# w2 of both FFNs by blocks: where the kept gates' product, silu and second product are called, and the second block unit of FFN 1

## The chip, the cores and the metric

The kernel runs on one core of one Trainium2 chip. Its metric is the device time of one execution in microseconds (us). Engines are named as in the profile: PE (TensorE, matmuls), DVE (VectorE), ACT (ScalarE), POOL (GpSimd) and SP (SyncE, which here only issues DMA transfers). Each engine works through its own instructions in the order in which the program issues them, and waits where an instruction's inputs or its buffer are not ready.

## The reference

One layer of a streaming encoder on 512 tokens of width 1024, all in float32: an FFN, a mixing block (a recurrent branch and windowed attention, gated), and a second FFN, with a norm ahead of and behind each.

```python
def swiglu(x, w1, w3, w2):
    return (jax.nn.silu(x @ w1) * (x @ w3)) @ w2
...
        f = swiglu(rms_norm(h, ffn1_pre_g[l]), ffn1_w1[l], ffn1_w3[l], ffn1_w2[l])
        h = h + 0.5 * rms_norm(f, ffn1_post_g[l])
        u = rms_norm(h, mix_pre_g[l])
        q, k, v, xr, xg = jnp.split(u @ w_in[l], splits, axis=-1)
...
        h = h + rms_norm(merged @ w_o[l], mix_post_g[l])
        f = swiglu(rms_norm(h, ffn2_pre_g[l]), ffn2_w1[l], ffn2_w3[l], ffn2_w2[l])
        h = h + 0.5 * rms_norm(f, ffn2_post_g[l])
```

The hidden width of an FFN is 2816, that is 22 tiles of 128, numbered f = 0 to 21.

## The kernel before

**Numbers in two parts.** Every float32 operand of a matmul is split into a high part (an ACT copy to the matmul's type) and a low part (source minus high part, on DVE). `split2` (L211) does this, and so do L178 and L179 for a weight tile. A product is then three matmuls: high by high, low weight by high, high weight by low. The high parts stand in the trace as `whi` or `[..]h`, the low parts as `wlo` or `[..]l`.

**Buffers.** Almost all tiles lie in one pool of 42 buffers of 4 KB per partition (`NSLOT`, L1673). A tile that is asked for takes a buffer that another tile leaves, and its first writer waits until that tile's last user is done. Banks for PE's results are 8.

**An FFN, first half (w1 and w3).** In FFN 1 the first tiles f = 0 to 3 (`NC1`) are computed one by one (`single`, L1164), in FFN 2 only 0 and 1 (`NC2`). All later tiles go through `Pairs` (L689): one job handles two tiles of one weight with seven half-size products in place of eight, so with sums of the weight's and the input's blocks made beforehand (`prep`, L706). A job of `Pairs.run` (L755) issues, in this order: product a11 and its copy q1 (L771), hook 1, product s1 and its copy q5 (L774), hook 2, then `last` of the job before (its product a22 and what follows it), product s2 and its copy u (L782), hook 3, product s4, product s3 and its copy v (L804), and in the last job of all a12 (`c11`) at this place. The a22 product of a job adds into the same bank that L804 reads. In the last job the silu of the job before (L785) and `tail` (L787) come right behind hook 3, and `tail` once more (L807) ahead of `c11`.

**The factor of FFN 1.** In FFN 1 the input of w1 and w3 is not yet normed: the factor per token (`Rb`, L1012) is computed beside the first matmuls and multiplied in later. So `last` of a w1 job copies the a22 result (L822), multiplies both tiles by the factor (L823, on DVE) and returns the silu of both tiles (L824, on ACT), which the next job calls. FFN 2's input is normed already: there `last` calls three silus on ACT (L826 to L828) and no product with a factor.

**Kept gates.** In FFN 1 the tiles f = 2 and 3 are done before the factor is there. `keep` (L1182) copies their raw results into a tile `kept`, and three steps are left for later: product with the factor (L1190, DVE), silu (L1191, ACT), and the product of silu and the w3 result (L1195, DVE).

**An FFN, second half (w2).** The hidden tiles 4 to 19 go through `Halves` (L518): w2 is multiplied by blocks, again seven products in place of eight, in 28 units of 12 matmuls (`unit`, L605), four for each of the products m1, m5, m2, m6, m7, m3, m4. `prep` (L573) makes one unit's operands: weights' high part (L591 or L587, ACT) and low part (L596 on DVE, or L593/L587 on ACT with an adding DMA from POOL), the hidden tile's split (L213 on ACT, L214 on DVE), and the sums that later units need (L548 and L551, DVE). The first units are made ready in the last pair job: hooks 1 and 2 and the two calls of `tail` make units 0 to 3. `run` (L636) then does, for each unit u: `prep` up to unit u + 4, the hooks of u, the matmuls of u, and after units 3, 7, 15 and 19 the copy or sum of the banks (`out`, L619; L629 is the ACT copy, L627 the DVE sum). The products m1, m6, m7 and m4 add into the same two banks (`BANK`, L524), so unit 16 waits for the copy after unit 15.

The hidden tiles that are left over, 0 to 3, 20 and 21, are the tail (`TAIL`, L1684): `RAW_TAIL` and `SPLIT_TAIL` (L1692) say at which units their weights are loaded and they and their weights are split, in the order that `TAIL` gives; `H_BACK` brings back the residual tiles h. `tok_gemm` (L366) then adds the tail's products token tile by token tile, in the same order, and norms each token tile (`norms`, L314), whose result is transposed on PE (L343). Ahead of that it asks for the next weights, `raw_xr` in FFN 1 (L413). In FFN 1 the softplus of a small vector (L1121) is hooked to unit 25.

Where the kept steps are called is set by these lines: each entry of `KEPT_AT` (L1685) is a unit, and the step goes ahead of the unit's other hooks.

```python
    for u, fn in zip(KEPT_AT, (gate_kept, swiglu_kept) * (NC1 - NG)):
        half.hooks[u].insert(0, lambda f=NG + KEPT_AT.index(u) // 2, fn=fn: fn(f))
```

Of the kernel before, what the change touches and what calls it, by code (L numbers as in the profile page):

```python
# [12 lines left out]
AF = mybir.ActivationFunctionType  # L13
ALU = mybir.AluOpType
# [37 lines left out]
def hybrid_layer(ctx: ExitStack, tc: tile.TileContext, a: dict, out: bass.AP):  # L52
    nc = tc.nc
    act, dve, pool, pe, sp = nc.scalar, nc.vector, nc.gpsimd, nc.tensor, nc.sync
# [8 lines left out]
    def slot(shape, dt=F32, name="s"):  # L63
        uid[0] += 1
        return sb.tile(shape, dt, tag="slot", name=f"{name}_{uid[0]}")
# [38 lines left out]
    def want(name, tiles):  # L104
        order.extend((name, i) for i in tiles)
# [3 lines left out]
    def want_ffn(na, nb, n):  # L109

        for i in range(n):
            order.extend([(na, i), (nb, i)])
        for i in range(n, FT, 2):
            paired.update(range(len(order), len(order) + 4))
            order.extend([(na, i), (na, i + 1), (nb, i), (nb, i + 1)])

    want_ffn("w1a", "w3a", NC1)
    want("w2a", TAIL)
    order += [("xr", i) for i in range(8)]
# [14 lines left out]
    want_ffn("w1b", "w3b", NC2)  # L134
    want("w2b", TAIL)

    st = {"dma": 0, "split": 0, "get": 0}
    raws, pairs = {}, {}
# [10 lines left out]
    def dma_to(n):  # L149
        while st["dma"] < min(n, len(order)):  # L150
            dma_one(st["dma"])
            st["dma"] += 1
# [11 lines left out]
    def split_to(n):  # L164
        while st["split"] < min(n, len(order)) and st["split"] not in paired:
            k = st["split"]
            dma_to(k + 1)
            r = raws.pop(k)
            if order[k] in BY_DMA:
                nm, i = order[k]  # L170
                pairs[k] = split_dma(r, a[nm][i * P : (i + 1) * P, :])
            else:
                hi = slot([P, D], F32R, name="whi")
                lo = slot([P, D], F32R, name="wlo")
                if order[k] in BY_POOL:
                    pool.tensor_copy(hi, r)
                else:
                    act.activation(hi, r, AF.Copy)  # L178
                dve.tensor_tensor(out=lo, in0=r, in1=f32(hi), op=ALU.subtract)  # L179
                pairs[k] = (hi, lo)  # L180
            st["split"] += 1
# [469 lines left out]
    def blocks(nm, hid, pairs, late, h_src):  # L651

        hooks = {u: [] for u in range(28)}

        def tail_tile(n):
            hid.to(n + 1)
            split_to(st["get"] + n + 1)

        def h_back(t):
            h[t] = slot([P, D], name="h")  # L660
            sp.dma_start(out=h[t], in_=h_src(t))

        for at_, fn in ((RAW_TAIL, lambda n: dma_to(st["get"] + n + 1)), (SPLIT_TAIL, tail_tile), (H_BACK, h_back)):
            for n, u in enumerate(at_):
                hooks[u].append(lambda n=n, fn=fn: fn(n))
        half = Halves(nm, hid, hooks)
        pairs.more = lambda n: half.load(LOAD_PAIRS[n])
        ahead = lambda: half.prep(half.ready + 1)
        end = len(pairs.jobs) - 1
        late[end, 1], late[end, 2] = [ahead], [ahead]  # L670
        pairs.run(ahead, late)
        return half

# [336 lines left out]

    hid, X1 = Hidden(TAIL), {}
    Rb = slot([P, 2, SEQ], name="Rb")  # L1012
# [134 lines left out]
    def uview(hh, th):  # L1147

        return lambda e, k: uT[:, e, 4 * hh + k, th * 256 : th * 256 + 256]
# [9 lines left out]
    def to_uT(src, hh, th):  # L1159
        v = [uT[:, e, 4 * hh : 4 * hh + 4, th * 256 : th * 256 + 256] for e in range(2)]  # L1160
        split2(v[0], v[1], src)
        return uview(hh, th)
# [17 lines left out]
    kept = {}  # L1180

    def keep(u):  # L1182
        f, i = u // 2, u % 2
        if f not in kept:
            kept[f] = slot([P, 2, SEQ], name="kept")
        act.activation(kept[f][:, i, :], ps[u], AF.Copy)

    def gate_kept(f):
        t = kept[f]
        dve.tensor_tensor(out=t[:, 0, :], in0=t[:, 0, :], in1=Rb[:, 0, :], op=ALU.mult)  # L1190
        act.activation(t[:, 0, :], t[:, 0, :], AF.Silu)  # L1191

    def swiglu_kept(f):
        t = kept.pop(f)
# [25 lines left out]
    late = {(0, 1): [lambda: keep(2 * NC1 - 1)], (1, 1): [bias_in], (2, 3): [bias_parts], (3, 1): [bias_rows]}  # L1220
    for i in range(P // 16):
        late[4 + i, 1] = [lambda i=i: bias_spread(i)]

    h.clear()
    half = blocks("w2a", hid, pairs_a, late, lambda t: a["x"][t * P : (t + 1) * P, :])
    X1 = pairs_a = late = None
    for u, fn in zip(KEPT_AT, (gate_kept, swiglu_kept) * (NC1 - NG)):
        half.hooks[u].insert(0, lambda f=NG + KEPT_AT.index(u) // 2, fn=fn: fn(f))
    half.hooks[SOFTPLUS_AT].append(softplus)
    xf = {(hh, th): slot([P, 4, 256], name="xf") for hh in range(2) for th in range(2)}  # L1230
    bs = tok_gemm(
        "w2a", hid, FT, len(TAIL), "ffn1_post_g", 0.5, "mix_pre_g", [("xr", i) for i in range(4)], xf=xf, spill=True, eps=veps, pre=half)
    half = None
# [376 lines left out]

    hid, tn = Hidden(TAIL), []
    X2 = {"b11": uview(0, 0), "b21": uview(1, 0), "b22": uview(1, 1)}
# [38 lines left out]
    late = {(0, 1): [lambda: X2.update(t4=to_uT(tn[3], 0, 1)), tn.clear]}  # L1651
    pairs_b.prep(1, 1)

    half = blocks("w2b", hid, pairs_b, late, lambda t: h_scr[t])
    X2 = pairs_b = None
    tok_gemm("w2b", hid, FT, len(TAIL), "ffn2_post_g", 0.5, None, [], pre=half)

# [23 lines left out]

BY_POOL = {("wg", i) for i in range(2, 8)} | {("wk", 0), ("wk", 1)}

TAIL = (0, 1, 2, 3, 20, 21)  # L1684
KEPT_AT = (15, 17, 18, 19)  # L1685
SOFTPLUS_AT = 25
LEAD = 5
U_SLOTS = 4
# [14 lines left out]
NC1 = 4  # L1703

NG = 2
# [55 lines left out]
```

## Time and profile before

| | before |
|---|---|
| median of 3 runs | 1123.17 us (1122.95 to 1123.32) |
| profiled execution | 1123.3 us |
| its span | 1121.5 us |
| granted clock of PE, mean | 0.990 |
| PE busy | 1101.1 us, 98% |
| DVE busy | 914.2 us, 82% |
| ACT busy | 669.2 us, 60% |
| POOL busy | 390.0 us, 35% |

The span runs from the first to the last instruction; the execution's time has 1.8 us more around it. Busy times are of the whole span: an engine with 82% can still be the one that is late in one stage, so the stage is what has to be read. A view of waits lists who waited for whom; a timeline lists the instructions of a stretch with the idle time before each; a view of windows gives busy time and granted clock of each engine in stretches that one chooses. FFN 1's w2 blocks lie between 237 and 324 us of the span, FFN 2's between 1004 and 1081 us.

### The profile page before, as it was taken

The page shows a single profiled execution, that of the slowest core. Times are in us where ns is not written, and L with a number is a line of the kernel's source. Part 1 is how long each engine was busy: PE and PEld are TensorE (multiplying, and loading weights), DVE is VectorE, ACT ScalarE, POOL GpSimd, SP SyncE. Part 2 cuts the span into 40 slices and gives each one's busy share as a digit, 9 for nine tenths or more (in the row PEclk, how much of TensorE's full clock was granted, in tenths as well). Part 3 has the DMA queues.
Part 4 walks back from the last instruction along what each step waited for, and adds up shares of the span by engine and source line. Part 5 has one row for each costly group of instructions (what it writes and reads, how often), then busy time and mean ns, then how long its engine had stood idle before and what let it go on. Part 6 is the DMA issues. An engine that isn't in the chain of part 4 may idle for free.

```text
span 1121.5 us, 17990 instructions
## 1 busy us (share of the span) xinstructions
PE 1101.1 (98%) x6850; PEld 993.1 (89%) x6850; DVE 914.2 (82%) x1337; ACT 669.2 (60%) x1175; POOL 390.0 (35%) x308
## 2 busy tenths in 40 slices
PE   9999999989799999999999999999999999999997
PEld 7899999978688877899888888888999999998885
DVE  5878999899778978888677866767889989589954
ACT  7755555557646677856556564356555555567821
POOL 0242532202111523033565664010877655602100
PEclk9999999989899999999999999999999999999999
DMA  9235653547762562136222245352323323376731
GB/s 351 101 97 132 149 117 112 177 162 161 176 226 86 177 170 94 57 120 236 99 93 76 94 169 207 105 197 85 141 76 113 113 76 114 111 241 147 190 120 75
DMA packets 52662, 155.41 MB, mean 139 GB/s; under 512 B 5456, under 2 KB 7376, under 8 KB 52576
## 3 DMA queue, kind: packets, MB, share of 16 engines
q1 hardware_dynamic: 42256, 129.57, 32.8%
q0 software_dynamic: 10032, 24.16, 10.7%
q8 instruction: 54, 0.88, 0.3%
q10 hardware_dynamic: 288, 0.52, 0.1%
q14 instruction: 32, 0.26, 0.1%
HBM read 138.52 MB, written 13.62 MB: 136 GB/s over the span
## 4 chain that ended last, share of the span: by engine, by line
PE 93%; DVE 5%; ACT 1%; issue 1%; DMA 0%; DVEq 0%; SPq 0%; ACTq 0%
PE c L683 13%; PE c L684 13%; PE c L685 13%; PE f L224 9%; PE f L225 9%; PE f L226 9%; PE hw L615 4%; PE hw L617 4%; PE hw L616 4%; PE acc L244 2%; PE acc L242 2%; PE acc L243 2%; PE hw L243 1%; PE hw L244 1%; PE hw L242 1%; DVE wlo L596 1%
## 5 line engine op out<-in xcount | busy, mean ns | idle before, releaser
L684 PE MATMUL c<-uT,wlo 128*128 128x256 f32 x516 | 146.0, 283 | 0.0
L685 PE MATMUL c<-uT,whi 128*128 128x256 f32 x516 | 146.0, 283 | 0.0
L683 PE MATMUL c<-uT,whi 128*128 128x256 f32 x516 | 146.0, 283 | 0.0
L683 PE MATMUL c<-Xh,whi 128*128 128x256 f32 x504 | 142.7, 283 | 0.0
L684 PE MATMUL c<-Xh,wlo 128*128 128x256 f32 x504 | 142.6, 283 | 0.0
L224 PE MATMUL f<-uT,whi 128*128 128x512 f32 (+1 forms) x368 | 136.4, 371 | 0.2 <-DVE o L1550 0.2
L225 PE MATMUL f<-uT,wlo 128*128 128x512 f32 (+1 forms) x368 | 134.8, 366 | 0.0
L226 PE MATMUL f<-uT,whi 128*128 128x512 f32 (+1 forms) x368 | 134.8, 366 | 0.0
L685 PE MATMUL c<-Xl,whi 128*128 128x256 f32 x456 | 129.1, 283 | 0.0
L214 DVE TENSOR_TENSOR wlo<-S,whi 128x1024 fp32r<-128x1024 f32 x86 | 118.8, 1381 | 6.8 <-ACT whi L213 3.3
L213 ACT ACTIVATE whi<-S 128x1024 fp32r<-128x1024 f32 x86 | 88.5, 1055 | 30.8 <-DVE S L732 29.7
L684 PEld LDWEIGHTS c<-uT,wlo 128*128 128x128 f32 x516 | 99.0, 192 | 0.2
L683 PEld LDWEIGHTS c<-uT,whi 128*128 128x128 f32 x516 | 99.0, 192 | 0.2
L685 PEld LDWEIGHTS c<-uT,whi 128*128 128x128 f32 x516 | 99.0, 192 | 0.0
L683 PEld LDWEIGHTS c<-Xh,whi 128*128 128x128 f32 x504 | 96.8, 192 | 0.3 <-issue 0.3
L684 PEld LDWEIGHTS c<-Xh,wlo 128*128 128x128 f32 x504 | 96.8, 192 | 0.0
L685 PEld LDWEIGHTS c<-Xl,whi 128*128 128x128 f32 x456 | 87.5, 192 | 0.0
L615 PE MATMUL hw<-whi,uT 128*128 128x512 f32 x192 | 76.0, 396 | 7.0 <-ACT hc L629 7.0
L224 PEld LDWEIGHTS f<-uT,whi 128*128 128x128 f32 x368 | 69.4, 189 | 12.7 <-issue 1.4
L226 PEld LDWEIGHTS f<-uT,whi 128*128 128x128 f32 x368 | 69.4, 188 | 11.5
L225 PEld LDWEIGHTS f<-uT,wlo 128*128 128x128 f32 x368 | 69.4, 189 | 10.8
L1503 POOL TENSOR_SCALAR P<-P,d 128x256 f32<-128x256 f32 (+1 forms) x64 | 62.0, 984 | 45.7 <-DVE d L1501 33.3
(434 smaller groups left out, 3199.3 us busy)
## 6 DMA issues: line engine op xcount, KB each, us to landing
raw_w2a<-in_w2a_dram SPq DMA_DIRECT2D x22, 512.0 KB, 4.1
raw_w1b<-in_w1b_dram SPq DMA_DIRECT2D x22, 512.0 KB, 4.1
raw_w3b<-in_w3b_dram SPq DMA_DIRECT2D x22, 512.0 KB, 4.3
raw_w2b<-in_w2b_dram SPq DMA_DIRECT2D x22, 512.0 KB, 4.5
raw_w3a<-in_w3a_dram SPq DMA_DIRECT2D x21, 512.0 KB, 4.3
raw_w1a<-in_w1a_dram SPq DMA_DIRECT2D x20, 512.0 KB, 4.2
raw_wg<-in_wg_dram SPq DMA_DIRECT2D x16, 512.0 KB, 3.8
h<-in_x_dram SPq DMA_DIRECT2D x8, 512.0 KB, 6.5
```

The costliest lines, as they stand in the source:

```text
L213: act.activation(hi, src, AF.Copy)
L214: dve.tensor_tensor(out=lo, in0=src, in1=f32(hi), op=ALU.subtract)
L224: pe.matmul(ps[:, c0:c1], wh[:, s], h_, start=k == 0 and c0 == 0, stop=False, skip_group_check=True)
L225: pe.matmul(ps[:, c0:c1], wl[:, s], h_, start=False, stop=False, skip_group_check=True)
L226: pe.matmul(ps[:, c0:c1], wh[:, s], l_, start=False, stop=k == KT - 1, skip_group_check=True)
L615: pe.matmul(ps, xs[:, 0, j, c], hi[:, j, :], start=start and j == 0, stop=False, skip_group_check=True)
L616: pe.matmul(ps, xs[:, 0, j, c], lo[:, j, :], start=False, stop=False, skip_group_check=True)
L617: pe.matmul(ps, xs[:, 1, j, c], hi[:, j, :], start=False, stop=u % 4 == 3, skip_group_check=True)
L683: pe.matmul(ps, wh[:, s], xh, start=first, stop=False, skip_group_check=True)
L684: pe.matmul(ps, wl[:, s], xh, start=False, stop=False, skip_group_check=True)
L685: pe.matmul(ps, wh[:, s], xl, start=False, stop=k == 3, skip_group_check=True)
L1503: pool.tensor_scalar(out=pt[:, x, b0:256], in0=pt[:, x, b0:256], scalar1=d[:, x : x + 1], scalar2=None, op0=ALU.mult)
```

## The change

Three edits. The second block unit that FFN 1 prepares inside the last pair job moves from hook 2 to hook 3, that is behind the product with the factor; FFN 2 keeps hook 2. The first product and the silu of a kept gate become two functions, and the six steps of the two kept gates, which were called at units 15, 17, 18 and 19, are called at units 18 and 19 (products with the factor), 21 and 22 (silus), 22 and 23 (second products). The order of the tail, for both FFNs, becomes 0, 1, 20, 21, 2, 3.

```diff
-        late[end, 1], late[end, 2] = [ahead], [ahead]
+        late[end, 1], late[end, 2 if pairs.R is None else 3] = [ahead], [ahead]
...
     def gate_kept(f):
-        t = kept[f]
-        dve.tensor_tensor(out=t[:, 0, :], in0=t[:, 0, :], in1=Rb[:, 0, :], op=ALU.mult)
-        act.activation(t[:, 0, :], t[:, 0, :], AF.Silu)
+        dve.tensor_tensor(out=kept[f][:, 0, :], in0=kept[f][:, 0, :], in1=Rb[:, 0, :], op=ALU.mult)
+
+    def silu_kept(f):
+        act.activation(kept[f][:, 0, :], kept[f][:, 0, :], AF.Silu)
...
-    for u, fn in zip(KEPT_AT, (gate_kept, swiglu_kept) * (NC1 - NG)):
-        half.hooks[u].insert(0, lambda f=NG + KEPT_AT.index(u) // 2, fn=fn: fn(f))
+    for fn, at_ in zip((gate_kept, silu_kept, swiglu_kept), KEPT_AT):
+        for f, u in zip(range(NG, NC1), at_):
+            half.hooks[u].insert(0, lambda f=f, fn=fn: fn(f))
...
-TAIL = (0, 1, 2, 3, 20, 21)
-KEPT_AT = (15, 17, 18, 19)
+TAIL = (0, 1, 20, 21, 2, 3)
+KEPT_AT = (18, 19), (21, 22), (22, 23)
```

## The prediction

> **What bounds the kernel now.** The page's first part puts TensorE (PE) at 1101.1 of the 1121.5 us span; nothing but PE's gaps, and stretches in which PE is slow, can be won. So I read the waits of PE first (who waited <- for whom: total us, times, longest).
>
> ```profile
> PE hw L615 <- ACT hc L629: 7.0, 1, 7.0
> PE c L683 <- ACT ct L804: 3.8, 1, 3.8
> ```
>
> Both lie in FFN 1, where the change acts; FFN 2, with the same code for pairs and blocks, has no such row. I then read the timeline around each. A row is start, duration, engine, line, operation, tiles; the bracket is the idle time before and what ended it. The 7.0 us first:
>
> ```profile
> 287.08 0.69 DVE L1190 TENSOR_TENSOR kept<-kept,Rb 128x512 f32<-128x512 f32 x1
> ...
> 287.81 0.63 ACT L1191 ACTIVATE kept<-kept 128x512 f32<-128x512 f32 x1 [8.78 <-DVE kept L1190]
> 288.34 1.07 ACT L629 ACTIVATE hc<-hw 128x512 f32<-128x512 f32 x2
> ...
> 288.97 0.80 PE L615 MATMUL hw<-whi,uT 128*128 128x512 f32 x1 [6.96 <-ACT hc L629]
> ```
>
> Block unit 16 adds into the banks that L629 copies out after unit 15, so PE must wait for the copy. The copy stands on ACT behind the silu of kept gate 2 (L1191), and this behind its product (L1190), which DVE reaches only after all the work queued before it: ACT idled 8.78 us for it. Unit 15 itself was done at 282.0 (288.97 - 6.96). Now the 3.8 us:
>
> ```profile
> 226.76 0.37 ACT L822 ACTIVATE cc<-c 128x256 f32<-128x256 f32 x1
> 231.59 1.06 ACT L824 ACTIVATE cc<-cc 128x1024 f32<-128x1024 f32 x1 [4.19 <-DVE cc L823]
> ...
> 233.50 0.61 ACT L213 ACTIVATE hx<-hEO 128x512 fp32r<-128x512 f32 x1
> 234.02 0.36 ACT L804 ACTIVATE ct<-c 128x256 f32<-128x256 f32 x1
> ...
> 226.86 1.22 DVE L596 TENSOR_TENSOR wlo<-raw_w2a,whi 128x1024 fp32r<-128x1024 f32 x1
> ...
> 229.74 0.69 DVE L551 TENSOR_TENSOR hEO<-hEO,hEO 128x512 f32<-128x512 f32 x1
> 230.34 1.22 DVE L823 TENSOR_TENSOR cc<-cc,Rb 128x1024 f32<-128x1024 f32 x1
> ...
> 234.43 0.58 PE L683 MATMUL c<-Xh,w 128*128 128x256 f32 x1 [3.82 <-ACT ct L804]
> ```
>
> The last a22 product needs the bank that L804 reads. L804 stands behind the silu L824, this waits for the factor product L823, and L823 stands on DVE behind the four operations of the second block unit (L596 to L551, 226.86 to 230.34), though its last input (L822) was there at 227.1.
>
> An idle PE also loses its clock. The windows give the granted clock as the column before the last two.
>
> ```profile
> 232.60:233.60 1.00, 0.00 (x0) 0.00 (x0) 0.00 (x0) 1.00 (x3) 0.00 (x0) 0.60 0.02 6
> 234.40:239.80 5.40, 5.37 (x19) 4.82 (x20) 5.40 (x9) 3.02 (x4) 0.00 (x0) 0.52 0.19 55
> ...
> 288.90:294.20 5.30, 5.23 (x12) 4.13 (x13) 2.89 (x4) 5.30 (x9) 1.85 (x2) 0.50 0.33 50
> ```
>
> The clock fell 2.2 us into the idle time (0.60 is 0.2 us at 1 and 0.8 at half, from 232.6; idle since 230.6) and stayed at half for some 5.3 us of work after either wait. That is 2.6 us each, beside the waits: 7.0 + 3.8 + 5.2 = 16.0 us is all that lies here.
>
> **The change, part by part.** *Second block unit behind the factor product.* No instruction is added; L591, L213 on ACT and L596, L214, L548, L551 on DVE go from hook 2 to hook 3 of the last pair job, past the a22 product of the job before, its copy L822 and the copy L782; the one load that they bring to SP's queue, the tenth of w2a, feeds unit 8 at the earliest. L823 then starts at about 226.9, when the first unit's DVE work ends, and ends at 228.0. ACT does L782, the moved L591 and L213, L824, the third unit's L591 and L213, L804, back to back from 226.4 (starts lie some 0.1 closer than the durations, so 1.5 for an L591 with its L213 and 1.0 for L824): L804 at 230.7 in place of 234.02, PE's a22 at 231.2. That leaves a wait of 0.5, too short for the clock. Its 12 matmuls took 2.73 at clock 0.52, so 1.4 at 1, and block unit 0 starts at 232.6.
>
> What is late next is DVE. FFN 2 shows it, because there nothing multiplies by the factor and PE does not stop:
>
> ```profile
> 222.02 0.38 ACT L771 ACTIVATE ct<-c 128x256 f32<-128x256 f32 x1 [0.54 <-PE c L685]
> ...
> 993.97 0.38 ACT L771 ACTIVATE ct<-c 128x256 f32<-128x256 f32 x1 [0.54 <-PE c L685]
> ...
> 1022.94 0.39 PE L615 MATMUL hw<-whi,uT 128*128 128x512 f32 x1
> 1023.94 0.50 PE L617 MATMUL hw<-whi,uT 128*128 128x512 f32 x1
> ...
> 1023.20 0.68 DVE L214 TENSOR_TENSOR uT<-hEO,uT 128x512 fp32r<-128x512 f32 x1
> ...
> 1048.31 0.50 PE L615 MATMUL hw<-whi,uT 128*128 128x512 f32 x1
> ...
> 1075.60 1.22 DVE L179 TENSOR_TENSOR wlo<-raw_w2b,whi 128x1024 fp32r<-128x1024 f32 x1
> ```
>
> The last pair jobs start 771.95 us apart (L771). DVE's order from there is FFN 2's, plus one L823 (1.13 from start to start of neighbours). FFN 2's unit 7 got its low part when L214 ended at 1023.88, and its third matmul went at 1023.94; here that is 253.1. PE alone would bring unit 7's third matmul at 232.6 + 7 x 2.72 + 0.45 = 252.1 (2.72 a unit: (321.48 - 294.26)/10, rows below). So DVE takes back 1.0 us over units 5 to 7, in pieces under 1 us. This makes the sum insensitive to the 0.5 above: up to 1 us more there costs nothing.
>
> ```profile
> 260.09 0.39 PE L615 MATMUL hw<-whi,uT 128*128 128x512 f32 x1
> ...
> 294.26 0.40 PE L615 MATMUL hw<-whi,uT 128*128 128x512 f32 x1
> ...
> 321.48 0.39 PE L615 MATMUL hw<-whi,uT 128*128 128x512 f32 x1
> ```
>
> Unit 8 starts at 253.1 + 2.27 = 255.4 where it was 260.09: 4.7 us. *The kept product leaves unit 15.* ACT is then free when unit 15 ends; the copy fits as in FFN 2, where unit 16 (1048.31) began 0.2 after its turn. So unit 16 at 255.4 + 8 x 2.72 + 0.2 = 277.4, unit 17 at 280.1 against 294.26: **14.2 us** up to here. The four kept instructions on DVE (0.6 from start to start) and two on ACT are the same; what hides them is DVE's lead. In FFN 2 unit 27's operands were ready long before its turn:
>
> ```profile
> 1072.65 0.69 DVE L214 TENSOR_TENSOR uT<-hEO,uT 128x512 fp32r<-128x512 f32 x1
> ...
> 1078.39 0.39 PE L615 MATMUL hw<-whi,uT 128*128 128x512 f32 x1
> ```
>
> Moved by 771.95, with 1.13 and three of the kept operations (1.8), L214 ends at 304.3, PE comes at 307.3: 3.0 us of lead, so PE pays nothing in these units; without the lead each kept operation would cost its 0.6. The new waits are harmless: behind a silu on ACT stand a unit's or a tail tile's conversions, but its product was issued three units earlier, and by DVE's order above the two are done near 289 and 292, while ACT comes to the silus at 291 and 293.
>
> *End of the stage.* DVE ends FFN 2's tail at 1076.8; minus 771.95, plus 1.13, plus four kept operations (2.4), plus softplus:
>
> ```profile
> 315.41 0.16 DVE L1126 TENSOR_SCALAR z<-z 128x8 f32<-128x8 f32 x1
> ...
> 320.04 0.70 DVE L1143 TENSOR_SCALAR bxh<-vec 64x8 f32<-64x8 f32 x4
> 320.77 0.69 DVE L214 TENSOR_TENSOR hT<-cc,hT 128x512 fp32r<-128x512 f32 x1
> ...
> 321.49 3.00 SPq L146 DMA_DIRECT2D raw_xr<-in_xr_dram  x3
> ...
> 318.84 1.06 ACT L178 ACTIVATE whi<-raw_xr 128x1024 fp32r<-128x1024 f32 x1 [5.27 <-DMA raw_xr<-in_xr_dram]
> ...
> 326.28 1.07 ACT L178 ACTIVATE whi<-raw_xr 128x1024 fp32r<-128x1024 f32 x1 [0.94 <-DMA raw_xr<-in_xr_dram]
> ...
> 332.56 0.69 DVE L294 TENSOR_TENSOR hc<-hw,hc 128x512 f32<-128x512 f32 x1 [3.35 <-PE hw L244]
> ...
> 339.34 0.75 DVE L333 SCALAR_TENSOR_TENSOR hg<-h,r,bc_mix_pre_g 128x512 f32<-128x512 f32 x1
> ...
> 340.52 1.03 PE L343 MATMUL tr<-ident,hg 128*128 128x128 f32 x8
> ```
>
> Softplus takes 5.3, so DVE ends at 313.7. PE ends unit 27 at 310.0 and wants the last tail tile, now kept gate 3, at 313.4: 0.3 late. DVE thus gains only 8.9 us where PE gains 14.2. The fourth raw_xr load was issued (321.49) when the last tail tile's split freed its buffer (L214, to 321.46); now that is 312.6. From 321.46 it took 7.1 us until DVE had that weight split and was at the first L294 (328.5); so 319.7, and the second L294 at 320.3 against 332.56 - 14.2 = 318.4. The chain to L333 had 0.4 to spare before the transposes (340.09 against 340.52). Loss: 1.5, the 0.3 included.
>
> *The tail's order, in both FFNs.* No instruction more or less; pair 20, 21 is split two places earlier, 2, 3 later, and a buffer comes free at other units. FFN 2 has no PE wait and I take 0. What a changed buffer can do is seen in the block loop's copies (idle before them, and who ended it):
>
> ```profile
> L591 ACT ACTIVATE whi<-raw_w2a 128x1024 fp32r<-128x1024 f32 x24 | 25.2, 1051 | 9.7 <-PE hw L616 3.7 <-PE hw L617 3.4 <-DVE uT L214 1.9
> ```
>
> They wait for buffers, up to 1.9 us at once, so each of these edits may cost or gain about 2 us; I keep both ends.
>
> *A rule beside it.* The Trainium skill (TensorE: Matmul & The Clock Gate, "What's actually happening") says that the clock is halved after an idle window of about 3.4 us and returns after about 3.4 us of work. The rows differ: 2.2 and 5.3. By its 3.4 us of half clock the two recoveries would give 3.4 us and not 5.2, and the forecast would be 1.8 us higher.
>
> **The sum.** 14.2 - 1.5 = 12.7 us. The profiled execution took 1123.3 us (span 1121.5 and 1.8 around it), the median is 1123.17, so the two scales agree to 0.1: **1110.6 us**. All later stages run on PE without a wait worth a row, and move as a whole.
>
> **The rivals.** *The next load is not late* (the fourth raw_xr gets a buffer earlier): nothing of the 1.5 is lost, perhaps also the 1.0 of units 5 to 7 not: 1107.5 to 1109. *The copy stays behind something else.* L629 still stands behind L591 and L213 of unit 19, and L591 there waited for a DVE L214. If its new buffer comes with unit 17's or 18's L214 (278 to 282 in the new times), the copy is 2 to 5 us late, and over 2.2 us the clock's 2.6 comes on top: 1113 to 1118. For it: the 1.9 in the row above; against it: FFN 2, where the same copy waits for PE alone. *The change doesn't do what it says* (the copy or L804 was held by buffers and the named waits only ended last): 1121 to 1125. Against it: the 8.78 and 4.19 name the products. *Slower: loads behind the kept tile.* SP issues in order. If one of the four h loads, and not the fourth raw_xr, gets kept gate 3's buffer, free at 312.6, then eight loads follow from there, one every 2.5 us ((326.28 - 318.84)/3), after 4.8 for the first: 334.8, then 2.9 for both splits and L294: 337.7, 5.1 later than before; less 0.4 spare, plus 2.6 of clock: 7 us slower, 1130. It decides against the change once more than five loads stand behind that buffer. Against it, the h loads were issued 13 us before the last tail tile was split:
>
> ```profile
> 308.07 3.52 SPq L661 DMA_DIRECT2D h<-in_x_dram  x4
> ```
>
> **How the numbers follow.** Forecast (1109 to 1113) 0.62; next load in time 0.12; copy still held 0.15; no effect 0.05; slower 0.06. The range 1107.5 to 1117.5 takes in the first three and their buffer terms, and leaves out about 0.14. A measurement of this kernel tells 0.2%, 2.2 us, from no change. Faster 0.89, within 0.05, slower 0.06.
>
> **What would show it.** Right: neither row of the first fence over 1 us; no window at half clock between 225 and 315; unit 17 at 280; DVE without a gap from 226 to 313; a wait of PE on L343's hg of 1 to 2 us. Wrong: L629 with a long bracket naming DVE; L615 waiting for whi or uT by more than 1 us; raw_xr issued after 315; any new PE wait in FFN 2.

## The result, and the profile after

| | before | after |
|---|---|---|
| median of 4 runs each | 1123.06 us (1122.88 to 1123.32) | 1110.70 us (1110.65 to 1110.95) |
| profiled execution, span | 1123.3, 1121.5 us | 1110.68, 1108.9 us |
| granted clock of PE, mean | 0.990 | 0.998 |
| DVE busy | 914.2 us | 912.5 us |

After takes 0.989 of the time of before (95% interval 0.9873 to 0.9907). Where did 12.6 us of span go? First all the waits of PE in the kernel after (who waited <- for whom: total us, times, longest):

```profile
PE w L990 <- POOL warm L987: 1.1, 1, 1.1
PE hw L243 <- DVE wlo L179: 0.7, 1, 0.7
PE c L683 <- ACT ct L804: 0.3, 1, 0.3
PE hw L616 <- DMA wlo<-in_w2b_dram: 0.3, 1, 0.3
```

The 7.0 us wait is gone and the 3.8 us one is 0.3. The first row lies at the start of the kernel. The second and the last are new: the last tail tile of FFN 1 (a product with kept gate 3), and block unit 23 of FFN 2. Now the timeline of after around both places (start, duration, engine, line, operation, tiles; bracket: idle time before, and who ended it):

```profile
226.91 1.22 DVE L823 TENSOR_TENSOR cc<-cc,Rb 128x1024 f32<-128x1024 f32 x1
228.16 1.06 ACT L824 ACTIVATE cc<-cc 128x1024 f32<-128x1024 f32 x1
230.59 0.36 ACT L804 ACTIVATE ct<-c 128x256 f32<-128x256 f32 x1
231.01 0.39 PE L683 MATMUL c<-Xh,w 128*128 128x256 f32 x1 [0.34 <-ACT ct L804]
232.54 0.40 PE L615 MATMUL hw<-whi,hx 128*128 128x512 f32 x1
...
253.16 0.51 PE L617 MATMUL hw<-whi,uT 128*128 128x512 f32 x1
255.56 0.39 PE L615 MATMUL hw<-whi,uT 128*128 128x512 f32 x1
...
275.33 1.06 ACT L591 ACTIVATE whi<-raw_w2a 128x1024 fp32r<-128x1024 f32 x1 [3.44 <-DVE uT L214]
276.30 0.61 ACT L213 ACTIVATE uT<-hEO 128x512 fp32r<-128x512 f32 x1
276.84 1.28 ACT L629 ACTIVATE hc<-hw 128x512 f32<-128x512 f32 x2
277.49 0.50 PE L615 MATMUL hw<-whi,uT 128*128 128x512 f32 x1
280.35 0.39 PE L615 MATMUL hw<-whi,uT 128*128 128x512 f32 x1
```

The factor product L823 comes right behind the first unit's work, ACT meets no wait before L804, unit 0 starts at 232.54. Unit 7's third matmul goes at 253.16, held back by DVE as in FFN 2, and unit 8 at 255.56. The copy L629 follows L213 with no bracket, and unit 17 is at 280.35: 13.9 us ahead of before. The chain that the prediction feared, a copy behind an L591 that waits for a buffer, is there all the same: L591 waited 3.44 us for DVE's L214, and ACT came to the copy only at 276.84. Unit 16 starts 0.39 us after the matmul before it, where matmuls in a row start 0.23 apart, so 0.16 us was lost. It was near.

The windows of after (stretch, then PE, PEld, DVE, ACT and POOL busy; granted clock; DMA's mean busy share; GB/s):

```profile
225.00:315.00 90.00, 88.70 (x413) 72.87 (x412) 89.18 (x134) 64.99 (x89) 16.49 (x15) 1.00 0.78 212
```

The clock is 1.00 throughout: the half-clock stretches are gone. And DVE is busy for 89.18 of 90 us: it now works nearly without a gap, as the prediction had it.

The end of the stage in after:

```profile
303.08 4.76 SPq L146 DMA_DIRECT2D raw_xr<-in_xr_dram  x3
307.55 0.39 PE L615 MATMUL hw<-whi,uT 128*128 128x512 f32 x1
...
311.24 1.58 DVE L1143 TENSOR_SCALAR bxh<-vec 64x8 f32<-64x8 f32 x4
311.38 2.79 POOL L410 TENSOR_SCALAR bc_mix_pre_g<-bc_mix_pre_g 128x1024 f32<-128x1024 f32 x1 [6.77 <-DMA bc_mix_pre_g<-in_mix_pre_g_dram]
...
313.45 1.22 DVE L179 TENSOR_TENSOR wlo<-raw_w2a,whi 128x1024 fp32r<-128x1024 f32 x1
314.59 4.62 DVE L179 TENSOR_TENSOR wlo<-raw_xr,whi 128x1024 fp32r<-128x1024 f32 x4
314.73 0.50 PE L243 MATMUL hw<-wlo,hT 128*128 128x512 f32 x1 [0.67 <-DVE wlo L179]
319.13 1.28 DVE L294 TENSOR_TENSOR hc<-hw,hc 128x512 f32<-128x512 f32 x2
327.60 1.03 PE L343 MATMUL tr<-ident,hg 128*128 128x128 f32 x8
```

DVE's row is unbroken: softplus, the last tail split, then four splits of the next weights in a row (4.62 us), then the first L294. PE waits 0.67 us at the last tail tile. The transposes start at 327.60 against 340.52: 12.9 us are gained at the end of FFN 1.

One thing in these rows can't be read from the order of the instructions. The four instructions of L1143, the end of softplus, took 0.70 us in before and 1.58 here: one of them, at 311.40, took 1.04 and the others 0.15 to 0.17. It started as POOL began L410 (311.38). Without this 0.88 us the last tail split would end at 313.79, ahead of PE, which comes to it at 313.90 (0.23 after the matmul at 313.67). In three other profiles, too, a DVE instruction beside L410's start is the long one: L1137 with 0.96 us in the whole with less lateness, L214 with 1.47 for 0.69 under the extra DVE operation, L1143 with 1.05 under the fourth low part (these experiments are below). That POOL holds DVE up there is argued from these rows; no run moves L410.

FFN 2 (units 0 and 27) takes 1065.79 - 990.67 = 75.12 us where it took 1078.39 - 1003.85 = 74.54:

```profile
990.67 0.40 PE L615 MATMUL hw<-whi,hx 128*128 128x512 f32 x1
...
1065.79 0.39 PE L615 MATMUL hw<-whi,uT 128*128 128x512 f32 x1
```

```profile
1003.85 0.40 PE L615 MATMUL hw<-whi,hx 128*128 128x512 f32 x1
```

(The second fence is before.) So 12.9 us at the end of FFN 1, less 0.6 in FFN 2, plus 0.3 gained between the two, make 12.6 us, the difference of the spans.

### The profile page after: what moved, and what is told of

It reads as the page before. It is cut to its first block, busy times and chain, and to the rows that moved or that the text cites. A ratio compares the mean times of both kernels' runs of the same rounds, so it can differ in the third digit from the quotient of the medians.

```text
span 1108.9 us, 17987 instructions
## 1 busy us (share of the span) xinstructions
PE 1098.4 (99%) x6850; PEld 989.6 (89%) x6850; DVE 912.5 (82%) x1337; ACT 668.9 (60%) x1175; POOL 389.9 (35%) x308
## 4 chain that ended last, share of the span: by engine, by line
PE 86%; DVE 10%; DMA 2%; issue 1%; ACT 0%; POOL 0%; DVEq 0%; SPq 0%; POOLq 0%; ACTq 0%
PE c L683 12%; PE c L684 12%; PE c L685 12%; PE f L224 9%; PE f L225 9%; PE f L226 9%; DVE wlo L596 2%; PE acc L243 2%; PE acc L244 2%; PE acc L242 2%; DVE uT L214 1%; DVE raw_w2a L548 1%; PE hw L243 1%; PE hw L244 1%; PE hw L242 1%
## 5 line engine op out<-in xcount | busy, mean ns | idle before, releaser
L683 PE MATMUL c<-uT,whi 128*128 128x256 f32 x516 | 146.1, 283 | 0.0
L683 PE MATMUL c<-Xh,whi 128*128 128x256 f32 x504 | 142.8, 283 | 0.0
L214 DVE TENSOR_TENSOR wlo<-S,whi 128x1024 fp32r<-128x1024 f32 x86 | 118.7, 1380 | 8.1 <-POOL OL L1557 4.5
L213 ACT ACTIVATE whi<-S 128x1024 fp32r<-128x1024 f32 x86 | 88.5, 1054 | 31.4 <-DVE S L732 29.7
L683 PEld LDWEIGHTS c<-uT,whi 128*128 128x128 f32 x516 | 99.1, 192 | 0.2
L683 PEld LDWEIGHTS c<-Xh,whi 128*128 128x128 f32 x504 | 96.8, 192 | 0.3 <-issue 0.3
L224 PEld LDWEIGHTS f<-uT,whi 128*128 128x128 f32 x368 | 69.4, 189 | 12.5 <-issue 1.7
L616 PE MATMUL hw<-wlo,uT 128*128 128x512 f32 x192 | 75.2, 392 | 0.4 <-DMA wlo<-in_w2b_dram 0.3
```

What stands on the lines that cost most here:

```text
L213: act.activation(hi, src, AF.Copy)
L214: dve.tensor_tensor(out=lo, in0=src, in1=f32(hi), op=ALU.subtract)
L224: pe.matmul(ps[:, c0:c1], wh[:, s], h_, start=k == 0 and c0 == 0, stop=False, skip_group_check=True)
L616: pe.matmul(ps, xs[:, 0, j, c], lo[:, j, :], start=False, stop=False, skip_group_check=True)
L683: pe.matmul(ps, wh[:, s], xh, start=first, stop=False, skip_group_check=True)
```

## The experiments

The theory: PE is the bound; the two waits and the clock lost in them are all that can be won; once they are gone, DVE sets the pace of units 0 to 7 and of the end of the stage. The rivals: the gains of the edits simply add; the tail's order or the exact units matter; another engine or the transfers, not DVE, are late next. Medians of before in these runs are 1123.42 to 1123.49 (1123.06 in the result), so times can be set beside each other.

**One edit at a time: the hook.** Before, with the second block unit behind the factor product, nothing else:

```diff
-        late[end, 1], late[end, 2] = [ahead], [ahead]
+        late[end, 1], late[end, 2 if pairs.R is None else 3] = [ahead], [ahead]
```

> The kernel before with the hook edit alone (second block unit at hook 3). Theory, DVE sets the pace from the pair jobs' end to the kept product: the 3.8 us wait falls to 0.3 to 0.5 and its half clock goes, but DVE comes to the kept product only 2.1 us earlier (L596 of unit 4 at 240.9 in place of 243.0), so the wait of unit 16 for the copy grows from 7.0 to about 10 and the time is 1121.0. Rival, the waits of PE add: 3.8 + 2.6 of clock are won, 1116.7, and the second wait stays at 7.0.

Measured: 1121.36 us, ratio 0.9983 (0.9973 to 0.9992). Waits of PE and timeline in this kernel:

```profile
PE hw L615 <- ACT hc L629: 9.4, 1, 9.4
```

```profile
285.24 0.67 DVE L1190 TENSOR_TENSOR kept<-kept,Rb 128x512 f32<-128x512 f32 x1
285.95 0.63 ACT L1191 ACTIVATE kept<-kept 128x512 f32<-128x512 f32 x1 [8.77 <-DVE kept L1190]
```

The first wait went to 0.4 us, as forecast, and the second grew from 7.0 to 9.4. PE came earlier to unit 16, but the product L1190 ends a chain on DVE, which came only 1.84 us earlier (287.08 to 285.24). A wait removed upstream is handed to the next one, if that is set by another engine.

**One edit at a time: the kept steps and the tail.** After, with the hook at 2 for both FFNs.

```diff
-        late[end, 1], late[end, 2 if pairs.R is None else 3] = [ahead], [ahead]
+        late[end, 1], late[end, 2] = [ahead], [ahead]
```

> The changed kernel with the hook edit undone (kept steps at separate units and the new tail order alone). Theory: the 7.0 us wait and its 2.6 us of half clock go, the 3.8 us wait stays; DVE's end of the stage comes 2.1 us later than with both edits and costs little, since PE is later too: 1113.7. Rival, the edits add: 12.4 less the first wait's 6.4, so 6.0 us, 1117.1.

Measured: 1118.3 us, ratio 0.9941 (0.992 to 0.9961), but the runs fall into two groups, 1113.7 and 1114.1, and 1118.3 to 1119.5. The profile is of the second:

```profile
PE c L683 <- ACT ct L804: 3.8, 1, 3.8
PE hw L616 <- DMA wlo<-in_w2a_dram: 2.0, 1, 2.0
```

```profile
301.30:303.70 2.40, 0.37 (x2) 0.00 (x0) 2.40 (x5) 0.65 (x2) 0.00 (x0) 1.00 1.03 392
303.70:307.90 4.20, 4.18 (x11) 3.31 (x12) 4.20 (x6) 3.35 (x6) 0.00 (x0) 0.59 1.02 414
```

The 7.0 us wait is gone and the 3.8 us one stands, as it should. A new wait is there: unit 23 needs its low part, which an adding transfer brings, and the DMA engines are full (share 1.03). The wait of 2.0 us costs the clock as well (0.59 in the 4.2 us behind it): units 22 and 23 together take 307.93 - 298.56 = 9.4 us (their first start to unit 24's) and not 2 x 2.72, 3.9 more. Without them the profiled run's 1118.4 would be 1114.5, near the first group; since that group has no profile, that it lacks the wait is argued, not shown.

**One edit at a time: the tail's order.**

```diff
-TAIL = (0, 1, 2, 3, 20, 21)
+TAIL = (0, 1, 20, 21, 2, 3)
```

> The kernel before with the tail's order alone (0, 1, 20, 21, 2, 3 in both FFNs; kept steps and hook as before). Theory: nothing in FFN 1, where the copy's wait is the same, and 0.6 us lost in FFN 2, where the changed kernel's unit 23 waits for its low part's transfer: 1123.7. Rival, the order itself is what relieves the tail: 1 to 2 us won, 1121.5.

Measured: 1122.9 us, ratio 0.9998 (0.9989 to 1.0008). Both old waits stand (7.8 and 3.8 us). FFN 2 takes 1077.72 - 1003.14 = 74.58 us between units 0 and 27, so the 0.6 us that after loses in FFN 2 does not come from the order alone, and my expectation of a loss there failed. The order is worth nothing by itself.

**Is it the product's place or the silu's?** Before, with product and silu parted into two functions, as the change does, and the first product still at unit 15; hook and tail are those of before. Gate 3's product moves from unit 18 to 17, the second products from 17 and 19 to 18 and 20. Of the edit the list of units is shown:

```diff
-KEPT_AT = (15, 17, 18, 19)
+KEPT_AT = (15, 17), (17, 19), (18, 20)
```

> The kernel before with the kept silu alone moved off unit 15: products stay at 15 and 17, silus go to 17 and 19, second products to 18 and 20; old tail order, old hook. Theory, the copy waits because ACT works in order and the silu stands ahead of it: the 7.0 us wait goes although the product stays where it was: 1113.7, as with the kept steps moved late. Rival, DVE's place for the product matters (it now stands before unit 20's work, not behind it): a wait of over 1 us for the copy or for a unit's operands stays, 1116 or more.

Measured: 1115.23 us, ratio 0.9926 (0.9911 to 0.994). The copy in the timeline:

```profile
281.61 1.28 ACT L629 ACTIVATE hc<-hw 128x512 f32<-128x512 f32 x2 [2.56 <-PE hw L617]
287.10 0.68 DVE L1189 TENSOR_TENSOR kept<-kept,Rb 128x512 f32<-128x512 f32 x1
```

The product comes as late as ever (287.10; 287.08 in before), but the copy no longer stands behind its silu and waits for PE alone. So it was ACT's order that cost the 7.0 us: not the product, but what was queued behind the instruction that waited for it. A new wait of 1.4 us, for the low part of unit 23, takes part of it back, and the time is 1.5 us above the forecast of 1113.7.

**The whole with less lateness.** After, with the steps of the previous experiment and the old tail:

```diff
-TAIL = (0, 1, 20, 21, 2, 3)
-KEPT_AT = (18, 19), (21, 22), (22, 23)
+TAIL = (0, 1, 2, 3, 20, 21)
+KEPT_AT = (15, 17), (17, 19), (18, 20)
```

> Hook edit and separate silu together, but the kept steps early (products at units 15 and 17, silus at 17 and 19, second products at 18 and 20) and the tail's old order: the change without its lateness. Theory, what counts is that the silu no longer stands ahead of the copy on ACT; where the product stands among DVE's work is worth nothing to PE: 1110.7, as the whole change, give or take 0.7. Rival, the late kept steps and the new order carry part of the 12.4 us: 1113 or more.

Measured: 1111.09 us, ratio 0.9895 (0.988 to 0.991), the same as after within the intervals. Two things make the result: the hook, and a silu that is not in the copy's way.

**Is DVE the bound?** After, with one more 128x1024 operation on DVE (the maximum of the factor tile with itself, which changes no value) in the last pair job:

```diff
+                    if self.R is not None:
+                        dve.tensor_tensor(out=self.R, in0=self.R, in1=self.R, op=ALU.max)
```

> The changed kernel with one more DVE instruction of 128x1024 (1.13 us from start to start; a maximum of the factor tile with itself, which changes no value) behind the fourth block unit's work. Theory, DVE is what PE now waits for, first in units 5 to 7 and again at the end of the stage: 1.1 us slower, 1111.8, with unit 7 some 1.1 us later. Rival, DVE's work is covered: 1110.7.

Measured: 1112.03 us, ratio 0.9902 (0.9887 to 0.9917); span 1110.1 against 1108.9. In its timeline unit 7's third matmul is at

```profile
254.23 0.50 PE L617 MATMUL hw<-whi,uT 128*128 128x512 f32 x1
```

1.07 us later than in after. A DVE operation there costs its whole length (1.13 us from start to start): DVE sets the pace of units 0 to 7.

**Is the clock's term real?** Before, with 52 idle matmuls of 128x240 on a zero tile between units 15 and 16, in the gap in which PE waits for the copy (the lines that make the tile are not shown):

```diff
+                if u == 15 and self.nm == "w2a":
+                    ps = bank("w")
+                    for _ in range(52):
+                        pe.matmul(ps[:, :240], keep_warm[:, :P], keep_warm, start=True, stop=True)
```

> The kernel before with 52 matmuls of 128x240 on a zero tile into a spare bank between units 15 and 16, some 5.8 us that lie in the 7.0 us wait; they compute nothing that is used. Theory, half of what the wait costs beyond itself is the clock: with PE kept at work unit 16 runs at full clock, 2.6 us faster than before, 1120.6, though PE does more. Rival, unit 16 is slow for another reason (its operands or banks): 1123.2 or more, with starts 0.43 us apart as before.

Measured: 1122.87 us, ratio 0.9994 (0.9985 to 1.0004): the expected gain did not come. The trace says why:

```profile
282.12 5.97 PE L645 MATMUL w<-gap 128*128 128x240 f32 x52
...
289.00 0.53 PE L615 MATMUL hw<-whi,uT 128*128 128x512 f32 x1 [0.91 <-ACT hc L629]
291.92 0.39 PE L615 MATMUL hw<-whi,uT 128*128 128x512 f32 x1
...
310.76 0.50 PE L616 MATMUL hw<-wlo,uT 128*128 128x512 f32 x1 [1.87 <-DMA wlo<-in_w2a_dram]
```

Unit 16 starts where it did (289.00; 288.97) and runs at full clock: unit 17 is at 291.92 and not at 294.26, so the clock's term, 2.3 us, is shown. Unit 23 then waits 1.87 us for its low part, and the clock falls again (0.76 from 310.7 to 317.7). In this execution, at 1124.74 us the slowest of the ten, the clock was won and more than given back 20 us later; that a shorter wait at unit 23 eats the gain in the others is likely, but they have no profile.

**Softplus away from DVE, to POOL.** After, with softplus's small instructions on POOL but for three on DVE:

```diff
-        dve.tensor_tensor(out=z[1], in0=z[1], in1=z[2], op=ALU.mult)
+        pool.tensor_tensor(out=z[1], in0=z[1], in1=z[2], op=ALU.mult)
...
```

> The changed kernel with most of the softplus (all but three of its small instructions, 5 us of DVE) on POOL, which is idle then. Theory, the transposes are late because DVE has the tail's splits, softplus and four weight splits in a row and only then the first norm: the 0.7 us wait of the last tail tile and about 0.4 us before the transposes go: 1109.5. Rival, the load of the next weights is what is late (as I had put it in the prediction): 1110.7.

Measured: 1115.82 us, ratio 0.9934 (0.9919 to 0.9949), 5 us slower than after. It does not answer the question, whether DVE's list is what makes the end late, since it added two waits on DVE and one of PE (3.1 us for hg at the transposes):

```profile
312.85 0.17 DVE L1136 SCALAR_TENSOR_TENSOR z<-z,z 128x8 f32<-128x8 f32 x1 [5.75 <-POOL z L1135]
...
323.94 0.69 DVE L299 SCALAR_TENSOR_TENSOR fg<-hc,bc_ffn_post_g 128x512 f32<-128x512 f32 x1 [3.34 <-DMA bc_ffn_post_g<-in_ffn_post_g_dram]
```

The one step left on DVE waited 5.75 us for POOL, and the transfer L281, which after issues at 299.85, came behind softplus on POOL's queue at 319.84. A step moved to another engine brings that engine's queue with it.

**Softplus earlier on DVE.** After, with Abs and Exp ahead of the Silu table and the 29 DVE instructions in six parts behind pair jobs 4 to 14:

```diff
+    for i in range(6):
+        late[4 + 2 * i, 3] = [lambda i=i: soft_part(5 * i)]
...
-    half.hooks[SOFTPLUS_AT].append(softplus)
```

> The changed kernel with the gate's softplus moved: its Abs and Exp run ahead of the Silu table's load, and its 29 small VectorE instructions go in six parts behind pair jobs 4 to 14 of the third part of FFN 1, so that none of them is left in unit 25 of FFN 1. Theory (VectorE is what the end of FFN 1 waits for): the 0.7 us that the last tail tile waited for VectorE goes, and the tail splits and the work on the residual start earlier; of the 6.0 us of softplus only what reached PE is won, 0.7 + 0.4 us: about 1109.5 us. Rival (VectorE has no room behind the pair jobs, or the loads of the residual end the stage): 1110.7 us or more.

Measured: 1111.79 us (1110.72 to 1112.34), ratio 0.9892 (0.9878 to 0.9907); the total missed, while the tail did what the theory says: no wait there, and the transposes come 329.14 - 310.10 = 19.04 us behind unit 27's start, as in before (340.52 - 321.48); in after it is 20.05. So what made DVE late at the end, the lengthened instruction of L1143 included, is worth 1.0 us. It was lost again at a place that I had not thought of, and in part at units 21 and 23 (0.56 and 0.36 us for low parts):

```profile
34.84 1.28 ACT L1128 ACT_TABLE_LOAD   x1
...
36.34 1.28 ACT L1074 ACT_TABLE_LOAD   x1
...
40.11 0.50 PE L225 MATMUL f<-uT,wlo 128*128 128x512 f32 x1 [0.77 <-DVE wlo L179]
```

A second table load stands ahead of a weight's split on ACT (at 37.75; 36.02 in after), and PE waits 0.77 us for that split; unit 0 starts 1.0 us later than in after. My rival, no room behind the pair jobs, fell as well: PE has no wait between 100 and 226 us.

**Less DVE work ahead of unit 7.** After, with the fourth unit's low part by a copy and an adding transfer, in both FFNs (the expectation thought of FFN 1 alone):

```diff
-LO_DMA = {("m2", i) for i in range(4)}
+LO_DMA = {("m2", i) for i in range(4)} | {("m1", 3)}
```

> The changed kernel with the low part of FFN 1's fourth block unit taken from VectorE's list of 128x512 subtractions and done as a ScalarE copy and an adding transfer, as some others are. Theory (VectorE sets the pace of units 0 to 7): the 1.13 us of that subtraction are won nearly whole, about 1.0 us, if the transfer lands ahead of the unit's third matmul at about 241: 1109.7 us. Rival (the transfer lands late): PE waits 1 to 3 us at that unit, 1111.5 to 1114 us.

Measured: 1110.44 us, ratio 0.9892 (0.9866 to 0.9917), again in two groups: 1108.39 and 1108.66, 1112.21 and 1113.84. The profile is of the lowest:

```profile
241.35 0.50 PE L616 MATMUL hw<-wlo,hx 128*128 128x512 f32 x1 [0.31 <-DMA wlo<-in_w2a_dram]
...
254.89 0.39 PE L615 MATMUL hw<-whi,uT 128*128 128x512 f32 x1
...
326.37 1.03 PE L343 MATMUL tr<-ident,hg 128*128 128x128 f32 x8
```

Where the transfer lands with only 0.31 us of wait, unit 8 starts 0.67 us earlier than in after and the transposes 1.23, and FFN 2 takes 73.77 us where after took 75.12 (span 1106.6). A transfer that lands later is the likely cause of the upper group, but no run of it was profiled: that stays open.

**Are the transfers next?** After, with one more load of 512 KB at unit 17, into a tile that nobody reads:

```diff
+    def extra():
+        sp.dma_start(out=slot([P, D], name="unused"), in_=a["x"][0:P, :])
+
+    half.hooks[17].append(extra)
```

> The changed kernel with one more 512 KB load from DRAM, issued by SP at unit 17 of FFN 1, into a tile that nobody reads. Theory (the transfers of FFN 2's last low parts are what is late next): unit 23 of FFN 2 waits 1.5 to 2.5 us for its low part where it waits 0.3 now, and more by the clock if the gap passes 2.2 us: 1112 to 1115 us. Rival (the transfers have room): 1110.7 us.

Measured: 1112.7 us (1112.43 to 1113.59), ratio 0.9903 (0.9888 to 0.9918); in its timeline, units 22 and 23:

```profile
294.92 0.50 PE L616 MATMUL hw<-wlo,uT 128*128 128x512 f32 x1 [0.55 <-DMA wlo<-in_w2a_dram]
...
298.79 0.50 PE L616 MATMUL hw<-wlo,uT 128*128 128x512 f32 x1 [0.85 <-DMA wlo<-in_w2a_dram]
```

(The expectation names FFN 2; the load and these waits lie in FFN 1, whose units 22 and 23 did not wait in after.) Unit 27 starts 2.0 us later than in after (309.58): the transfers of the low parts have no room left in this stage. The transposes come only 1.0 us later (328.63), since the last tail tile no longer waits; most of the rest of the 2.0 us in the medians' difference lies in this profile in FFN 2, where unit 23 waits 0.6 us and no load was added.

**Both DVE reliefs.** The moved softplus and the fourth low part together, that is the diffs of these two experiments.

> The moved softplus and the fourth unit's low part by an adding transfer, together. If both are what VectorE's pace costs, they add: 1110.7 - 1.2 - 1.0 = 1108.5 us. If the transfers of the low parts are late next, unit 23 of FFN 2 takes it back: 1110.0 us or more.

Measured: 1110.93 us (1110.84 to 1111.52), ratio 0.9887 (0.9872 to 0.9902): the same as after, and not the sum. The gains are there (unit 8 at 255.87 although unit 0 starts 1.3 us later than in after; 19.04 us from unit 27 to the transposes), the table load costs its wait again, unit 23 of FFN 1 waits 0.35 us for its low part, and FFN 2's unit 23 0.5. None of these versions is shown to beat the changed kernel.

## Why the prediction was right, and where it was not

| step | predicted | measured |
|---|---|---|
| wait of L683 on L804 | 0.5 us | 0.34 us |
| unit 0 starts | 232.6 | 232.54 |
| unit 7's third matmul | 253.1 | 253.16 |
| unit 16, unit 17 | 277.4, 280.1 | 277.49, 280.35 |
| gained up to unit 17 | 14.2 us | 13.9 us |
| DVE ends the last tail split | 313.7 | 314.67 |
| last tail tile late by | 0.3 us | 0.67 us |
| fourth raw_xr issued | 312.6 | by 307.8 |
| second L294 | 320.3 | 319.7 |
| lost at the end of FFN 1 | 1.5 us | 1.0 us |
| FFN 2 | 0 | -0.6 us |
| in all | 12.7 us | 12.6 us |

**Both waits** had the cause that the brackets named: each kernel with one edit loses just the wait whose bracket the edit answers. What carried the sum was to ask for each wait who is late next: DVE, with FFN 2's schedule as the picture of it. The extra DVE operation shows it. **The clock's term** of the second wait was real: predicted at 2.6 us for unit 16's wait, it shows as 294.26 - 291.92 = 2.3. That of the first wait was not tested by itself.

**The failed step** is the fourth raw_xr load. The prediction held that it waits for kept tile 3's buffer and is issued at 312.6. In the trace the three loads behind the first go out in one row from 303.08 to 307.84, so the last did not wait for the split at 312.84 to 313.53 that frees that buffer. The first L294 was late all the same, because DVE had the last tail split and four weight splits ahead of it: 313.45 + 1.14 + 4.54 = 319.13 (start to start). Two different chains end within 0.6 us of each other, and the number came out nearly right for a wrong reason. DVE's own list should have been counted to the L294, not only to the last tail tile. And the late L294 cost PE nothing: the wait of L343 on hg, which the prediction announced with 1 to 2 us, was not there, because L333 ended at 327.25 and PE, late itself by then, came to the transposes at 327.60. All of the 1.0 us was lost at the last tail tile: from unit 27 to that tile's first matmul PE takes 6.12 us in before and after, from there to the transposes 12.92 in before (327.60 to 340.52) and 13.93 in after (313.67 to 327.60). DVE was 1.0 us later there than forecast, and 0.88 of it is the one lengthened instruction of L1143, which no list of instructions shows.

**The sum is nearer than its terms, and that is luck.** Against the forecast, 0.3 us are missing up to unit 17, 0.5 are saved at the end of FFN 1, 0.6 are lost in FFN 2, and 0.3 are gained between the stages, from nothing that the prediction names. Together they leave 0.1.

**The tail's order at 0** held. **A new PE wait in FFN 2**, which the prediction named as a sign against it, did appear, with 0.3 us and 0.6 us of time. It is not fixed by the code: FFN 2's code is the same in after, with the kept steps and the tail alone, and with softplus earlier, and in the last two FFN 2 takes 74.51 and 74.48 us without such a wait. With the new order (and FFN 2's code otherwise as in after) seven profiles show 74.48, 74.51, 74.58, 74.94, 75.08, 75.12 and 75.83, with the old one five show 74.48 to 74.55. So the low part's transfer lands sooner or later from one execution to the next; whether the order makes a late one likelier stays open.

**What the prediction had not seen** is that the two gains aren't independent: 2.1 us for the hook alone, 5.2 us for the rest alone (9.4 and 9.8 in two of its five runs), 12.4 together (medians). The plainest pair differs by the hook only: on top of the silu's experiment it brings 1115.23 - 1111.09 = 4.1 us, twice what it brings alone. The hook alone moves its gain into the next wait; the rest alone, in the execution that was profiled, runs into the low parts' transfers. The windows of before and after show how little room these have (columns as above):

```profile
280.00:310.00 30.00, 23.04 (x91) 18.48 (x91) 24.13 (x30) 20.83 (x30) 4.85 (x4) 0.83 0.74 181
```

```profile
280.00:310.00 30.00, 30.00 (x134) 24.86 (x133) 29.45 (x51) 21.62 (x31) 5.34 (x6) 1.00 0.98 283
```

In before, PE's stall at unit 16 gave the DMA engines time; in after their share is 0.98.

## What to carry to other kernels

An instruction that waits blocks all that stands behind it on its engine: when an urgent copy is late, look for what is ahead of it in its queue, and move the waiting one, not what it waits for. Value a stall by what is late next, counted to the end of the stage on every engine, and then on the DMA engines: two edits at two stalls of one stage can be worth more together than apart, and less than their waits. An edit that moves a step past a queue must pay for everything in that queue, a table load or a broadcast transfer too.

## What the runs showed of the hardware

- **A wait of less than 2 us can halve the clock, and the fall can come after PE is at work again.** A wait of 1.4 us at unit 23 left the clock at 1.00 (the experiment on the silu's place, window from 303.2 to 306.0). One of 1.87 us (idle matmuls) and one of 2.05 us (kept steps and tail alone) were followed by half clock, which began 2.9 and 2.7 us after PE fell idle, when it had worked again for 1.1 and 0.6 us. In the two long waits of before it began 2.2 and 2.0 us after PE fell idle.
- **The stretches at half clock have set lengths.** Worked out from the shares of the windows at their edges, the clock was at half from 311.82 to 315.24 with the idle matmuls, from 304.34 to 307.76 with the kept steps and the tail alone, and from 232.79 to 239.62 and 284.00 to 294.23 in before: 3.42, 3.42, 6.83 and 10.23 us, that is once, once, twice and three times 3.41. So the time from the end of a wait to full clock (4.0 to 5.3 us here) depends on where in such a stretch the wait ends; the prediction's 5.3 us is no constant. The Trainium skill (TensorE: Matmul & The Clock Gate, "What's actually happening") puts the idle window before the fall and the busy one before the return at about 3.4 us each. The lengths agree with that; the idle time does not, since 1.87 us were enough, and there the measurement decides.

```profile
303.20:306.00 2.80, 2.73 (x12) 2.26 (x13) 2.80 (x4) 2.77 (x6) 0.00 (x0) 1.00 0.98 369
```

```profile
311.20:312.00 0.80, 0.80 (x5) 0.67 (x4) 0.80 (x2) 0.79 (x2) 0.00 (x0) 0.89 1.02 338
...
315.00:316.00 1.00, 1.00 (x5) 0.77 (x5) 0.83 (x6) 0.00 (x0) 0.38 (x1) 0.88 1.01 414
```

(The first fence is the silu's experiment, the second the idle matmuls: 0.89 of 0.80 us is 0.62 us at full clock and 0.18 at half, so the fall is at 311.82.)

- **Adding transfers fill the DMA engines at a lower rate.** In after the four adding transfers of the low parts (512 KB each) are issued from 279.36 to 286.71 and take 5.9 to 10.0 us to land; from 288 to 296 us the engines' share is 1.12 with 207 and 232 GB/s. In the second experiment, from 303.70 on, when the last low part has landed and the loads are plain, it is 1.02 with 414 GB/s. From issue to use the last low part took 10.6 us where unit 23 waited for it in the silu experiment, 12.5 in the second.

```profile
288.00:292.00 4.00, 4.00 (x19) 3.30 (x19) 4.00 (x6) 4.00 (x7) 0.00 (x0) 1.00 1.12 207
292.00:296.00 4.00, 4.00 (x20) 3.30 (x19) 4.00 (x7) 4.00 (x6) 0.00 (x0) 1.00 1.12 232
```
